# Attention by pairs of query blocks: two items per round, and a head's values ahead of the turning

## The chip, the cores and the metric

The kernel runs on one core of one Trainium2 chip. The core has engines that run side by side, each with its own queue in order: TensorE (matmuls, "PE" in the profile; its weight loads are "PEld"), VectorE ("DVE"), ScalarE ("ACT"), GpSimd ("POOL") and SyncE ("SP", which here only issues DMAs). The metric is device time of one execution in microseconds (us); lower is better. A profiled execution also gives a trace with start and length of every instruction.

## The reference

A hybrid encoder block: RMS norm, one input projection, stick-breaking attention and a gated linear recurrence (HGRN2) side by side on the same input, a gated merge, an MLP with squared ReLU and a last norm. Sequence 1024, width 1024, 8 attention heads of 64. What matters here is the attention, cut to its core:

```python
def block(args):                      # one block of 128 queries
    qi, i = args
    qpos = i * Q_BLOCK + jnp.arange(Q_BLOCK)
    z = jnp.einsum('bhqd,bhkd->bhqk', qi, k) * scale
    mask = kpos[None, :] < qpos[:, None]
    log_beta = jax.nn.log_sigmoid(z)
    log_rem = jnp.where(mask, log_beta - z, 0.0)
    between = lax.cumsum(log_rem, axis=3, reverse=True) - log_rem
    w = jnp.where(mask, jnp.exp(log_beta + between), 0.0)
    return jnp.einsum('bhqk,bhkd->bhqd', w, v)
```

So the weight of a key is a sigmoid times the product of what all later keys left over.

## The kernel before, in words

The kernel is written with a tile framework: the program states instructions and tiles, and a scheduler, when the program is built, fixes the order on each engine and gives each tile a place. Big SBUF tiles ([128, 1024]) come from a pool of 40 slots, [128, 512] tiles from a pool of 10 halves, and PSUM has 8 banks of [128, 512]. A tile that finds no free place waits until the last reader of an older one is done.

TensorE's order is bound by two lanes. `pe` (called by `matmul`, L121, and by `turn`, L821) chains each instruction behind the last one of its lane; `open_block` says which lane is open. "main" holds the attention's own products, "fill" the projections that are worked off beside it. A fill block must come behind the main block that ended two blocks ago (`AHEAD = 2`); otherwise the scheduler merges the lanes freely. `st.advance(n, upto)` emits n steps of fill (a step is two blocks of contraction, six matmuls of 512 columns, for most projections), `st.finish(j)` all steps up to job j.

An item is one head and one block of 128 queries. The 64 items go head by head, in each head in the order 7, 0, 6, 1, 5, 2, 4, 3 of query blocks, so that items with many keys (even places) and few keys (odd places) alternate. An item of query block qb has nk = (qb + 1) * 128 keys. It goes through four functions:

- `scores`: on TensorE z = q k in two products (QH and QL, high and low part), in banks of at most 512 keys; ScalarE writes two sigmoids of it, `rm` (L758) and `bt` (L761); POOL clears the last column of `bt` (L762).
- `weights`: VectorE scans `rm` from the last key to the first (L781) and multiplies it into `bt` (L157); SyncE copies the result by DMA to a new tile `wr` (L791). `weighted` remembers the last multiplication; the low part of a projection's keys (in `qk_epilogue`) is ordered behind it on VectorE.
- `turn`: TensorE transposes `wr` in blocks of 128 keys into a bank `pw` (L821), up to four blocks per bank; ScalarE copies the bank to `wT` (L144). It returns the head when all eight items of the head are turned.
- `values`: TensorE multiplies a head's `wT` with the values into two banks `po`, 44 records; ScalarE (L872, L874) and VectorE (L875) put them together in `osb`.

Before the loop, items 0 to 2 are scored and items 0 and 1 weighted. In iteration i the loop weights item i + 2, scores item i + 3, emits one or two steps of fill and turns item i. A head's `values` are emitted in the first turn of the next head: `turn` of query block 7 turns its upper four blocks, calls `between`, which runs `values`, and turns its lower four. `next(wsums)` (every second item) puts one transfer of the output weights on POOL's queue. `attended` holds the last `weighted` back for the splits of later weights.

Of the kernel before, what the change touches and what calls it, by code (L numbers as in the profile page):

```python
# [22 lines left out]
NT = T // P  # L23
# [16 lines left out]
def kernel(  # L40
# [37 lines left out]
    def slot_n(name, n, dt=F32):  # L78

        if n <= 512:  # L80
            return hpool.tile([P, 512], dt, tag="h", name=name)
        return slot(name, dt)

    def bank(name):
        return psum.tile([P, 512], F32, tag="p", name=name)
# [17 lines left out]
    def open_block(name):  # L103
        cur[0] = name
        lane = lanes[name]
        lane.gates = (lane.last,)
        if name == "main":
            lane.ends.append(lane.last)
        else:
            ends = lanes["main"].ends  # L110
            lane.gates += tuple(ends[-AHEAD : len(ends) - AHEAD + 1])
# [8 lines left out]
    def matmul(*a, **k):  # L120
        return pe(nc.tensor.matmul(*a, **k))  # L121
# [10 lines left out]
    last_lo, attended, silu = [None], [None], [None]  # L132
# [23 lines left out]
    def mul(out, a, b):  # L156
        return nc.vector.tensor_tensor(out=out, in0=a, in1=b, op=ALU.mult)  # L157
# [138 lines left out]
    def norm_transpose(acts, half, b0, n, between=None):  # L296
# [15 lines left out]
        if between:  # L312
            between()
# [210 lines left out]
    st = Stream()  # L524
# [200 lines left out]
    j_qk = {0: j_first}  # L725
# [9 lines left out]
    items = [(h, qb) for h in range(NHS) for qb in QB_ORDER]  # L735
    zs, wTt, seen = {}, {}, {}
    lastsel, weighted = [None], [None]

    def scores(h, qb):
        open_block("main")  # L740
        nk = (qb + 1) * P
        QH, QL, KS = qk[h]
        bt, rm = slot_n(f"bt{h}_{qb}", nk), slot_n(f"rm{h}_{qb}", nk)
        step = 320 if nk == 640 else 512
        for s0 in range(0, nk, step):
            m = min(nk - s0, step)
            n = max(m, 256)
            z = bank(f"z{h}_{qb}_{s0}")
            for i, Q in enumerate((QH, QL)):
                matmul(  # L750
                    z[:, :n],
                    Q[:, qb * P : (qb + 1) * P],
                    KS[:, s0 : s0 + n],
                    start=i == 0,
                    stop=i == 1,
                )
            c0, e = int(s0 == 0), m - (s0 + m == nk)
            nc.scalar.activation(  # L758
                rm[:, s0 + c0 - 1 : s0 + m - 1], z[:, c0:m], AF.Sigmoid, scale=-0.125
            )  # L760
            nc.scalar.activation(bt[:, s0 : s0 + e], z[:, :e], AF.Sigmoid, scale=0.125)  # L761
        lastsel[0] = nc.gpsimd.memset(bt[:, nk - 1 : nk], 0.0)  # L762
        zs[h, qb] = (bt, rm)
# [6 lines left out]
    def weights(h, qb):  # L770

        nk = (qb + 1) * P
        bt, rm = zs[h, qb]
        cut = qb == NT - 1
        parts = ((512, nk - 1), (0, 512)) if cut else ((0, nk - 1),)
        wr = slot_n(f"wr{h}_{qb}", nk, F32R)
        for i, (a, b) in enumerate(parts):
            rr = rm[:, a:b][:, ::-1]  # L780
            nc.vector.tensor_tensor_scan(  # L781
                out=rr,
                data0=rr,
                data1=bits[:, 1024 - nk + a : 1024 - nk + b][:, ::-1],
                initial=rm[:, b : b + 1] if i else 0.0,
                op0=ALU.mult,
                op1=ALU.max,
            )
            weighted[0] = mul(bt[:, a:b], bt[:, a:b], rm[:, a:b])
            cs = slice(a, nk if i == 0 else b)  # L790
            nc.sync.dma_start(wr[:, cs].bitcast(F32), bt[:, cs])  # L791
        zs[h, qb] = wr

    def turn(h, qb, between):

        open_block("main")
        wr = zs.pop((h, qb))
        qc, par = qb // 2, qb % 2
        nkb = 2 * qc + 2
        if (h, qc) not in wTt:  # L800
            wTt[h, qc] = [
                slot_n(f"wT{h}_{qc}_{k0}", 256 * min(nkb - k0, 4)).rearrange(
                    "p (k q) -> p k q", q=256
                )
                for k0 in range(0, nkb, 4)
            ]
        tiles = wTt[h, qc]
        qs = slice(par * P, (par + 1) * P)
        order = list(enumerate(tiles))
        for i, t in order[::-1] if qb == NT - 1 else order:  # L810
            n = min(qb + 1 - 4 * i, 4)
            if n <= 0:
                continue
            if qb == NT - 1 and i == 0:
                between()
                open_block("main")
            pw = bank(f"pw{h}_{qb}_{i}")
            for kb in range(n):
                s0 = (4 * i + kb) * P
                pe(  # L820
                    nc.tensor.transpose(  # L821
                        pw[:, kb * P : (kb + 1) * P].bitcast(F32R), wr[:, s0 : s0 + P], ident_r
                    )
                )
            hi_copy(t[:, 0:n, qs], pw[:, : n * P].rearrange("p (k q) -> p k q", q=P))
            turn_hi[0] = hi_last[0]
        seen[h] = seen.get(h, 0) + 1
        return (h,) if seen[h] == NT else None

    def values(h):  # L830


        open_block("main")
        whole, left, right = slice(0, 256), slice(0, P), slice(P, 256)
        pair, r = h // 2, (h % 2) * DHS
        if pair not in osb:
            osb[pair] = slot(f"osb{pair}")
        other = DHS - r
        pos = []
        for big in (3, 2):  # L840
            po = bank(f"po{h}_{big}")
            order = []
            for kb in range(0, 2 * big, 2):
                order += [(big, kb, 0, whole), (big, kb + 1, 1, whole)]
            order += [(big, 2 * big, 0, left), (big, 2 * big, 1, right)]
            few = 3 - big
            order += [(few, 0, 0, whole), (big, 2 * big + 1, 1, right)]
            if few:
                order += [(few, 1, 1, whole), (few, 2, 0, whole)]
            order += [(few, 2 * few + 1, 1, right)]  # L850
            ends = {}
            for i, (qc, kb, half, cs) in enumerate(order):
                ends.setdefault((qc, half), [i, i])[1] = i
            for i, (qc, kb, half, cs) in enumerate(order):
                c0 = 0 if qc == big else 256
                first, last = ends[qc, half]
                matmul(
                    po[half * DHS : (half + 1) * DHS, c0 + cs.start : c0 + cs.stop],
                    v_stat(h, kb),
                    wTt[h, qc][kb // 4][:, kb % 4, cs],  # L860
                    start=i == first,
                    stop=i == last,
                )
            pos.append((big, po))
        for big, po in pos:
            tmp = slot_n(f"ot{h}_{big}", 512)
            for qc, c0 in ((big, 0), (3 - big, 256)):
                wTt.pop((h, qc))
                n0 = P if qc == 0 else 0
                cs = slice(c0 + n0, c0 + 256)  # L870
                dst = osb[pair][r : r + DHS, qc * 256 : (qc + 1) * 256]
                nc.scalar.copy(tmp[r : r + DHS, cs], po[other : other + DHS, cs])  # L872
                if n0:
                    nc.scalar.copy(dst[:, 0:n0], po[0:DHS, c0 : c0 + n0])  # L874
                nc.vector.tensor_tensor(  # L875
                    out=dst[:, n0:],
                    in0=po[r : r + DHS, cs],
                    in1=tmp[r : r + DHS, cs],
                    op=ALU.add,
                )  # L880
# [1378 lines left out]
    n_fill = 9 * (j_hg[0] - j_qk[0]) + 18  # L2259
    n_first = 3  # L2260
    ready = deque()
    wsums = out_weight_sums()
    done = 0
    for i, it in enumerate(items):
        if i + 2 < len(items):
            weights(*items[i + 2])
        if i + 3 < len(items):
            st.finish(j_qk[items[min(i + 5, len(items) - 1)][0]])
            scores(*items[i + 3])
        if i % 2 == 1:  # L2270
            next(wsums, None)
        want = n_first + (i + 1) * (n_fill - n_first) // len(items)
        st.advance(want - done, j_hg[1])
        done = want
        before = ready.popleft() if ready else None

        def between():
            if before:
                values(*before)

        r = turn(*it, between)
        if i == len(items) - 2:
            attended[0] = weighted[0]
        if it[1] != NT - 1:
            between()
        if r:
            ready.append(r)
    while ready:
# [123 lines left out]
```

## Time and profile before

| | us |
|---|---|
| median of 3 runs | 1412.3 (1411.65 to 1412.98) |
| the profiled execution | 1413.22 |
| its span, first to last instruction | 1411.1 |
| TensorE busy | 1399.3 |
| VectorE, ScalarE, POOL busy | 1003.1, 684.3, 154.9 |

The attention loop takes the span from about 50 to 310 us; the linear recurrence, the merge and the output projection follow up to about 810, then the MLP. A matmul's record ends by a model, and the records of neighbours overlap, so a busy TensorE says little; the time from one start to the next says what an instruction took. Engine waits are given as "idle before <- what released it".

### The profile page before, as it was taken

What the parts mean: (1) busy time and instruction counts of PE and PEld (TensorE: products, weight loads), DVE (VectorE), ACT (ScalarE), POOL (GpSimd) and SP (SyncE); (2) the same over time, 40 slices, a digit from 0 to 9 for tenths busy, and PEclk for the clock granted to TensorE, in tenths of its full rate; (3) what the DMA queues carried; (4) which work ended last, traced back from release to release, by engine and by line L of the source; (5) the groups of instructions that cost most, each with busy time, mean ns of one, the idle gap of its engine ahead of it and who ended that gap; (6) DMA issues with size and microseconds to landing.
All of it is one profiled execution on the core that took longest, in us unless ns stands there. A gap on an engine that the chain in (4) does not pass through costs nothing. (4 is left out here: it accounts for less than half of the span.)

```text
span 1411.1 us, 22762 instructions
## 1 busy us (share of the span) xinstructions
PE 1399.3 (99%) x8782; PEld 1177.2 (83%) x8782; DVE 1003.1 (71%) x1332; ACT 684.3 (48%) x1207; POOL 154.9 (11%) x315
## 2 busy tenths in 40 slices
PE   9999999999999999999999999999999999999997
PEld 8888888988988888888888888888888888888886
DVE  6587687667556885966768896667666657768665
ACT  7576676644244453423354854444544433433343
POOL 3121121110112231000010200000000000000042
PEclk9999999999999999999999999999999999999999
DMA  7357365664254894555695524444436964686824
GB/s 213 97 169 194 113 166 152 141 156 135 69 163 137 261 252 159 187 183 177 202 297 179 194 86 146 149 165 164 151 134 241 362 239 173 259 292 229 285 92 176
DMA packets 166916, 258.94 MB, mean 183 GB/s; under 512 B 27500, under 2 KB 91544, under 8 KB 166808
## 3 DMA queue, kind: packets, MB, share of 16 engines
q1 hardware_dynamic: 148120, 205.31, 43.0%
q0 software_dynamic: 14080, 43.00, 11.7%
q10 hardware_dynamic: 4608, 9.18, 1.9%
q8 instruction: 69, 1.13, 0.3%
q14 instruction: 39, 0.32, 0.1%
HBM read 167.79 MB, written 70.78 MB: 169 GB/s over the span
## 5 line engine op out<-in xcount | busy, mean ns | idle before, releaser
L781 DVE TENSOR_TENSOR_SCAN rm<-rm,bits 128x511 f32<-128x511 f32 (+7 forms) x72 | 87.3, 1221 | 35.9 <-ACT rm L758 35.7
L144 ACT CAST whid<-w 128x1024 fp32r<-128x1024 f32 x30 | 31.6, 1053 | 155.0 <-PE pm L121 90.7
L121 PE MATMUL pm<-wlod,sh 128*128 128x512 f32 x240 | 93.5, 390 | 0.0
L121 PE MATMUL pm<-whid,sh 128*128 128x512 f32 x240 | 93.4, 389 | 0.0
L121 PE MATMUL pm<-whid,sl 128*128 128x512 f32 x240 | 93.4, 389 | 0.0
L121 PE MATMUL pm<-tl,sh 128*128 128x512 f32 (+1 forms) x210 | 81.3, 387 | 0.0
L121 PE MATMUL pm<-th,sl 128*128 128x512 f32 (+1 forms) x210 | 81.3, 387 | 0.0
L121 PE MATMUL pm<-th,sh 128*128 128x512 f32 (+1 forms) x210 | 81.3, 387 | 0.0
L149 DVE TENSOR_TENSOR wlod<-w,whid 128x1024 fp32r<-128x1024 f32 x30 | 36.7, 1222 | 59.3 <-ACT whid L144 59.3
L149 DVE TENSOR_TENSOR sl<-sa,sh 128x1024 fp32r<-128x1024 f32 x56 | 68.2, 1217 | 0.8 <-ACT sh L144 0.8
L2061 POOL TENSOR_SCALAR fss<-fss 128x1 f32<-128x1 f32 x8 | 4.5, 561 | 561.9 <-ACT fsc L2056 561.3
L144 ACT COPY wT<-pw 128x128 f32<-128x128 f32 (+3 forms) x96 | 44.1, 484 | 34.1 <-PE pw L821 28.6
L144 ACT CAST sh<-sa 128x1024 fp32r<-128x1024 f32 x56 | 57.2, 1046 | 5.2 <-DMA sa<-ad 3.7
L157 DVE TENSOR_TENSOR bt<-bt,rm 128x511 f32<-128x511 f32 (+7 forms) x72 | 48.9, 686 | 8.8 <-ACT bt L761 2.8
L121 PEld LDWEIGHTS pm<-wlod,sh 128*128 128x128 f32 x240 | 45.0, 188 | 9.8 <-DVE wlod L149 0.4
L121 PEld LDWEIGHTS pm<-whid,sh 128*128 128x128 f32 x240 | 45.1, 188 | 9.5
L121 PEld LDWEIGHTS pm<-whid,sl 128*128 128x128 f32 x240 | 45.0, 187 | 9.2
L758 ACT ACTIVATE rm<-z 128x511 f32<-128x511 f32 (+4 forms) x96 | 48.4, 506 | 4.5 <-DMA wr<-bt 2.4
L121 PE MATMUL pX<-sql,t1h 128*128 128x512 f32 x128 | 50.0, 391 | 0.4 <-DVE sql L149 0.3
L761 ACT ACTIVATE bt<-z 128x512 f32<-128x512 f32 (+3 forms) x96 | 48.7, 509 | 3.5 <-DMA wr<-bt 2.6
L121 PE MATMUL pX<-sqh,t1h 128*128 128x512 f32 x128 | 49.8, 389 | 0.0
L121 PE MATMUL pX<-sqh,t1l 128*128 128x512 f32 x128 | 49.8, 389 | 0.0
(922 smaller groups left out, 4346.6 us busy)
## 6 DMA issues: line engine op xcount, KB each, us to landing
w<-in_w_ff_dram SPq DMA_DIRECT2D x72, 512.0 KB, 4.6
sa<-ad SPq DMA_DIRECT2D x56, 512.0 KB, 6.7
ad<-a SPq DMA_DIRECT2D x32, 256.0 KB, 4.1
ad<-s SPq DMA_DIRECT2D x16, 512.0 KB, 3.1
tw<-in_w_out_dram POOLq DMA_DIRECT2D x24, 256.0 KB, 4.3
wr<-bt SPq DMA_DIRECT2D x24, 256.0 KB, 3.2
pr<-pd SPq DMA_DIRECT2D x10, 512.0 KB, 6.4
x<-in_x_dram SPq DMA_DIRECT2D x8, 512.0 KB, 9.2
```

The lines of the kernel that those rows point to most:

```text
L121: return pe(nc.tensor.matmul(*a, **k))
L144: hi_last[0] = after(in_turn("act", nc.scalar.copy(dst, src)), hi_behind[0])
L149: nc.vector.tensor_tensor(out=dst, in0=src, in1=hi.bitcast(F32), op=ALU.subtract),
L157: return nc.vector.tensor_tensor(out=out, in0=a, in1=b, op=ALU.mult)
L758: nc.scalar.activation(rm[:, s0 + c0 - 1 : s0 + m - 1], z[:, c0:m], AF.Sigmoid, scale=-0.125)
L761: nc.scalar.activation(bt[:, s0 : s0 + e], z[:, :e], AF.Sigmoid, scale=0.125)
L781: nc.vector.tensor_tensor_scan(out=rr, data0=rr, data1=bits[:, 1024 - nk + a : 1024 - nk + b][:, ::-1], initial=rm[:, b : b + 1] if i else ...
L2061: nc.gpsimd.tensor_scalar(out=ssq, in0=ssq, scalar1=1.0 / D, scalar2=EPS, op0=ALU.mult, op1=ALU.add)
```

## The change

The loop goes over pairs. Round i (even) weights item i + 2, scores items i + 3 and i + 4, weights item i + 3, emits the fill of two items, runs the values of the head that the round before completed, and turns items i and i + 1. `turn` no longer takes `between`, and all its banks follow each other. `finish` looks one item further (i + 6 instead of i + 5), as the round scores up to item i + 4. `next(wsums)` comes once per round, and `attended` is set at the head of the last round.

```diff
-    def turn(h, qb, between):
+    def turn(h, qb):
...
-            if qb == NT - 1 and i == 0:
-                between()
-                open_block("main")
             pw = bank(f"pw{h}_{qb}_{i}")
...
-    for i, it in enumerate(items):
+    for i in range(0, len(items), 2):
         if i + 2 < len(items):
             weights(*items[i + 2])
-        if i + 3 < len(items):
-            st.finish(j_qk[items[min(i + 5, len(items) - 1)][0]])
-            scores(*items[i + 3])
-        if i % 2 == 1:
-            next(wsums, None)
-        want = n_first + (i + 1) * (n_fill - n_first) // len(items)
+            st.finish(j_qk[items[min(i + 6, len(items) - 1)][0]])
+            for it in items[i + 3 : i + 5]:
+                scores(*it)
+            weights(*items[i + 3])
+        else:
+            attended[0] = weighted[0]
+        next(wsums, None)
+        want = n_first + (i + 2) * (n_fill - n_first) // len(items)
         st.advance(want - done, j_hg[1])
         done = want
-        before = ready.popleft() if ready else None
-
-        def between():
-            if before:
-                values(*before)
-
-        r = turn(*it, between)
-        if i == len(items) - 2:
-            attended[0] = weighted[0]
-        if it[1] != NT - 1:
-            between()
+        if ready:
+            values(*ready.popleft())
+        for it in items[i : i + 2]:
+            r = turn(*it)
         if r:
             ready.append(r)
```

## The prediction

> **What bounds the kernel now.** I read the page first, then the windows by stage, then what TensorE waited for, then the timeline of TensorE inside attention.
>
> ```profile
> PE 1399.3 (99%) x8782; PEld 1177.2 (83%) x8782; DVE 1003.1 (71%) x1332; ACT 684.3 (48%) x1207; POOL 154.9 (11%) x315
> ...
> PEclk9999999999999999999999999999999999999999
> ```
>
> TensorE is busy for 1399.3 of 1411.1 us at full clock, and the clock row has no dip. So anything that does not shorten TensorE's own sequence can at best remove the few places where it stops. Attention runs from about 50 to 310 us:
>
> ```profile
> 50.00:310.00 260.00, 258.75 (x1738) 222.37 (x1738) 189.08 (x240) 170.64 (x407) 44.82 (x125) 1.00 0.58 153
> 310.00:771.00 461.00, 460.76 (x3864) 385.64 (x3864) 326.26 (x490) 188.90 (x337) 60.37 (x99) 1.00 0.59 186
> ```
>
> Columns after the length are busy time (and count) of PE, PEld, DVE, ACT and POOL, then clock, DMA share and GB/s. In attention VectorE has 189 and ScalarE 171 of 260 us, so neither is the bound. The next stage is as full on TensorE (460.76 of 461), so a microsecond won in attention is passed on to the end, and so is one lost. What TensorE waited for between 40 and 320 us is one row of 0.8 us (for the values' PSUM bank) and one of 0.4 us (for a landed weight tile):
>
> ```profile
> PE pjv L121 <- DVE osb L875: 0.8, 1, 0.8
> PE pw L821 <- DMA wr<-bt: 0.4, 1, 0.4
> ```
>
> Busy time hides more, because matmul records overlap. So I compare starts. One iteration today is turn, scores, fill:
>
> ```profile
> 199.68 0.64 PE L821 MATMUL pw<-ident_r,wr 128*128 128x128 f32 x6
> 200.15 0.46 PE L121 MATMUL z<-KS,QH 128*128 128x512 f32 x1
> 200.45 0.39 PE L121 MATMUL z<-KS,QL 128*128 128x512 f32 x1
> 200.68 0.40 PE L121 MATMUL z<-KS,QH 128*128 128x512 f32 x1
> 200.91 0.40 PE L121 MATMUL z<-KS,QL 128*128 128x512 f32 x1
> 201.15 0.39 PE L121 MATMUL pjqk<-xnh,wqk7h 128*128 128x512 f32 x1
> ```
>
> Columns are start, length, instruction. A 512-wide product takes 0.23 us from start to start, but the first score behind the transposes takes 0.30. Six transposes take 0.47, 0.078 each. A score block that follows fill pays nothing (0.23 at once):
>
> ```profile
> 49.84 0.40 PE L121 MATMUL z<-KS,QH 128*128 128x512 f32 x1
> 50.07 0.40 PE L121 MATMUL z<-KS,QL 128*128 128x512 f32 x1
> 50.31 0.39 PE L121 MATMUL z<-KS,QH 128*128 128x512 f32 x1
> ```
>
> So leaving a run of transposes costs 0.07 to 0.08 us. That is the one thing in TensorE's sequence that the change touches.
>
> **The change, part by part.** *Seams from transposes to scores.* Today scores(4) to scores(63) each follow a turn: 60 seams. With two turns and two scores per round the scores of rounds 2 to 60 follow turns: 30 seams. The price over the whole stage, from the groups by shape:
>
> ```profile
> L121 PE MATMUL z<-KS,QH 128*128 128x512 f32 x40 | 17.9, 447 | 0.0
> L121 PE MATMUL z<-KS,QL 128*128 128x512 f32 x40 | 15.7, 393 | 0.0
> ...
> L121 PE MATMUL z<-KS,QH 128*128 128x256 f32 x24 | 7.7, 322 | 0.0
> ...
> L121 PE MATMUL z<-KS,QL 128*128 128x256 f32 x24 | 6.7, 281 | 0.0
> ...
> L121 PE MATMUL z<-KS,QH 128*128 128x384 f32 x16 | 5.8, 365 | 0.0
> L121 PE MATMUL z<-KS,QL 128*128 128x384 f32 x16 | 5.4, 338 | 0.0
> L121 PE MATMUL z<-KS,QH 128*128 128x320 f32 x16 | 5.4, 342 | 0.0
> L121 PE MATMUL z<-KS,QL 128*128 128x320 f32 x16 | 4.8, 307 | 0.0
> ```
>
> QH and QL do the same work; QH is longer by 2.2 + 1.0 + 0.4 + 0.6 = 4.2 us. Over 60 seams that is 0.07 each, as in the timeline. Thirty fewer: 2.1 us by the groups, 2.4 by 0.08 from the timeline. I take **-2.2 us**.
>
> [...]
>
> ```profile
> 286.30 0.80 PEld L821 LDWEIGHTS pw<-ident_r,wr 128*128 128x128 f32 x7
> ...
> 287.05 0.19 PEld L121 LDWEIGHTS z<-KS,QH 128*128 128x128 f32 x1
> 287.08 0.38 PE L121 MATMUL z<-KS,QH 128*128 128x320 f32 x1
> ```
>
> The scores' load starts at 287.05, 0.03 us ahead of its own matmul and behind the whole chain of transposes' loads. [...]
>
> *Seams to fill.* At the tail three turns go straight to fill, at the same price (0.30, then 0.23):
>
> ```profile
> 294.34 0.46 PE L121 MATMUL pjq<-xnh,wq1h 128*128 128x512 f32 x1
> 294.64 0.39 PE L121 MATMUL pjq<-xnl,wq1h 128*128 128x512 f32 x1
> 294.87 0.40 PE L121 MATMUL pjq<-xnh,wq1l 128*128 128x512 f32 x1
> ```
>
> In pairs one such seam is left of three: -0.1 us.
>
> *Values ahead of the turning.* Today the values sit between the two halves of a head's first turn:
>
> ```profile
> 182.14 0.46 PE L821 MATMUL pw<-ident_r,wr 128*128 128x128 f32 x4
> 182.53 4.12 PE L121 MATMUL po<-wT,V 128*64 128x256 f32 x44
> 186.58 0.54 PE L821 MATMUL pw<-ident_r,wr 128*128 128x128 f32 x4
> ```
>
> Four transposes ahead of the values take 0.39, 0.08 above 4 x 0.078. Seven of eight such seams go (-0.5); the way from values back to transposes stays. In their place stands fill to values, which no row shows: between nothing (fill to scores, above) and 0.08 each, or 0.6 in all. A gain below nothing is excluded, since the 44 records themselves stay. I take the middle, +0.3.
>
> *Where scores, weights and forced fill move.* Per round VectorE gets the same scans, ScalarE the same sigmoids, SyncE the same `wr` transfers, POOL the same memsets and `tw` transfers, one `next(wsums)` per round instead of per second item; none of it adds work. `finish` now looks two items ahead of the second score, and forces three steps of head 1's projection early instead of one; steps taken early are only missing later, where fill is plentiful. Cost nothing; without that cover each step is 6 x 0.23 = 1.4 us.
>
> *The added wait.* weights(i+3) now stands directly behind scores(i+3) and scores(i+4), so its scan waits for ScalarE within the round, and behind it on VectorE wait the projections' low parts (ordered after `weighted`), then the `Q` copies on POOL. The item is turned one round later, behind two fills of about four steps (2 x 24 x 0.23 = 11 us) plus turns and scores: some 13 us, against the 12.1 us between these two rows for item 63 today:
>
> ```profile
> 290.61 0.47 PE L121 MATMUL z<-KS,QH 128*128 128x512 f32 x1
> ...
> 302.68 0.51 PE L821 MATMUL pw<-ident_r,wr 128*128 128x128 f32 x4 [0.42 <-DMA wr<-bt]
> ```
>
> The even items get another round, about 20 us. So the turn should not come to wait oftener than now. The stops of today are 1.14 us where 0.17 is due, in front of this row (the z before it starts at 125.46 and is 384 wide):
>
> ```profile
> 125.46 0.34 PE L121 MATMUL z<-KS,QL 128*128 128x384 f32 x1
> 126.60 0.35 PE L121 MATMUL pjv<-wv1h,xnh 128*128 128x256 f32 x1 [0.81 <-DVE osb L875]
> ```
>
> (384 of 512 columns of 0.23), so 1.0, and the 0.4 in front of the last turn: 1.4 us together. In pairs such stops lie between none and several us (the slot rival prices those), since one round with values now wants more banks within 3 us: two for `po`, three for the turns, three for the scores and one for fill, nine of eight. I take 1.7, near the rows of today, so +0.3.
>
> *Sum:* -2.2 - 0.1 - 0.5 + 0.3 + 0.3 = **-2.2 us**. The profiled execution took 1413.2 us (span 1411.1 and 2.1 around it), which would become 1411.0; the median of the three runs is 1412.3, and from it I forecast **1410.1 us**.
>
> **The rivals.** *The stops go as well.* If values, turns and scores in longer blocks give the banks back in time, the 1.4 us of stops and my 0.3 vanish: -2.5 - 1.4 = -3.9, 1408.4. For it: ScalarE is idle for a third of the stage. Against: nine banks of eight.
>
> [...]
>
> *Slower: SBUF holds the second score up.* The pair needs one more `bt`, `rm` and `wr` at a time, out of 40 slots. ScalarE already waits for a slot at the second item of heads 6 and 7:
>
> ```profile
> ACT bt L761 <- DMA wr<-bt: 2.6, 1, 2.6
> ACT rm L758 <- DMA wr<-bt: 2.4, 1, 2.4
> ```
>
> TensorE did not stop for these. In pairs the weight tile that would free the slot is read only at the round's end, one fill of 24 x 0.23 = 5.5 us later, so such a wait becomes 2.5 + 5.5 = 8 us with two score banks held, ScalarE's queue stuck, and the copies that free the other banks behind it. Cover is one fill, 5.5 us, so each costs TensorE some 2.5 us. One such wait eats the gain; from two on beyond what the seams give (-2.5 + 5 = +2.5) it is slower, with three 1412.3 + 5 = 1417. [...]
>
> **How the numbers follow.** The forecast case (1409 to 1411.5) has 0.44, the stops gone 0.19, the change without effect 0.16, the slots 0.21. About 0.2%, or 2.8 us, is what a measurement can tell from no change. Faster than that (under 1409.5): all of the second case and 0.21 of the first, 0.40. Slower (over 1415.1): 0.19 of the slots. Within: 0.41. The range goes from 1407.6, just under the case without stops, to 1416, short of three slot waits; about 0.1 is left out on each side. The forecast's own range is 1409.0 to 1411.5.
>
> **What would show it.** Right: pairs of `pw` groups with no score between them, QH longer than QL by about 2.1 instead of 4.2 us in all, values starting behind fill. The slots: new rows "PE <- ACT" or "PE <- DMA wr" and ScalarE waits for `wr` above 5 us. Without effect: fill between two `pw` groups of a round. The prediction is wrong if TensorE's starts show more than 3 us of new stops in attention, or if a later stage loses what attention wins.

## The result and the profile after

| | before | after |
|---|---|---|
| median, us (6 runs each) | 1412.45 (1411.57 to 1414.26) | 1422.18 (1421.40 to 1424.23) |
| span of the profiled execution | 1411.1 | 1420.1 |
| TensorE busy | 1399.3 | 1402.1 |

The ratio is 1.0071, with a 95% interval of 1.0058 to 1.0084: 9.7 us slower, where 2.2 us faster was forecast. TensorE does the same work (8782 records in both). What it waited for, in the view of its waits after the change (us in total, times, longest):

```profile
PE z L121 <- DVE osb L872: 3.7, 1, 3.7
...
PE z L121 <- ACT bt L761: 1.6, 1, 1.6
PE z L121 <- ACT v L914: 1.2, 2, 0.7
```

All are waits of a score (`z`) for something that is not its operand. VectorE's addition of the values (`osb`) and ScalarE's sigmoids and copies (`bt`, `v`) are the readers of older PSUM banks, and a score needs a free bank to write to. So these are waits for a bank. In attention TensorE's timeline has them at these places (start, length, instruction):

```profile
116.68 0.40 PE L121 MATMUL z<-KS,QH 128*128 128x512 f32 x1
116.92 0.39 PE L121 MATMUL z<-KS,QL 128*128 128x512 f32 x1
118.92 0.39 PE L121 MATMUL z<-KS,QH 128*128 128x256 f32 x1 [1.62 <-ACT bt L761]
...
277.38 0.28 PE L121 MATMUL z<-KS,QL 128*128 128x256 f32 x1
278.40 0.50 PE L121 MATMUL z<-KS,QH 128*128 128x512 f32 x1 [0.74 <-ACT v L914]
...
288.94 0.31 PE L121 MATMUL z<-KS,QL 128*128 128x320 f32 x1
292.98 0.61 PE L121 MATMUL z<-KS,QH 128*128 128x320 f32 x1 [3.73 <-DVE osb L872]
293.39 0.47 PE L121 MATMUL z<-KS,QL 128*128 128x320 f32 x1
293.65 0.63 PE L121 MATMUL pjq<-xnh,wq1h 128*128 128x512 f32 x1
294.08 0.63 PE L121 MATMUL pjq<-xnl,wq1h 128*128 128x512 f32 x1
...
298.67 0.39 PE L121 MATMUL pjq<-xnh,wq1h 128*128 128x512 f32 x1
298.90 0.39 PE L121 MATMUL pjq<-xnl,wq1h 128*128 128x512 f32 x1
```

Each of these stops, and a fourth of 0.6 us at 255 us, stands in front of a bank of the round's second score. From 293.65 the 512-wide products start 0.43 us apart instead of 0.23: the granted clock had gone from 1.00 to 0.50 during the stop of 4 us, at 291.7 us by windows of 0.2 us. The windows show it (length, busy PE, PEld, DVE, ACT, POOL, then clock, DMA share, GB/s):

```profile
286.00:292.00 6.00, 3.25 (x33) 2.54 (x29) 1.80 (x3) 0.15 (x2) 0.80 (x2) 0.98 0.94 262
292.00:293.00 1.00, 0.02 (x1) 0.05 (x1) 0.34 (x2) 0.94 (x4) 1.00 (x5) 0.50 0.70 265
293.00:298.60 5.60, 5.60 (x14) 4.54 (x15) 4.05 (x6) 3.74 (x10) 2.04 (x4) 0.51 0.92 164
298.60:304.00 5.40, 5.40 (x30) 4.54 (x30) 1.45 (x3) 2.68 (x6) 0.00 (x0) 1.00 0.42 125
```

Why did the bank come free so late at 292? VectorE's timeline, and ScalarE's:

```profile
290.08 0.69 DVE L1214 TENSOR_TENSOR wga8r<-wga8r,wga8r 128x512 f32<-128x512 f32 x1 [4.88 <-DMA wga8r<-in_w_in_dram]
290.81 0.69 DVE L1214 TENSOR_TENSOR wga8r<-wga8r 128x512 f32<-128x512 f32 x1
291.53 0.42 DVE L872 TENSOR_TENSOR osb<-po,ot 64x256 f32<-64x256 f32 x1
```

```profile
285.77 0.37 ACT L869 COPY ot<-po 64x256 f32<-64x256 f32 x1 [2.91 <-PE po L121]
291.99 0.26 ACT L869 COPY ot<-po 64x128 f32<-64x128 f32 x1 [5.84 <-DVE osb L872]
```

VectorE took its instructions in order: the first addition, whose copy ScalarE had ready at 286.14 us (285.77 + 0.37), started at 291.53, behind both differences. These two, of a gate's weights (`wga8r`) that nobody needs yet, stand in front of the additions and wait 4.9 us for a load of 512 KB, issued at 283.10 us; from 286 to 292 us the DMA engines' share is 0.94. Behind them the additions of head 6 wait, ScalarE's next copy waits for the additions (5.8 us), and the `po` bank that the second score is to take stays full.

At 278 us ScalarE's queue is what holds a bank. One of its sigmoids waits 3.3 us for a transfer of `wr`, which is the wait for an SBUF slot that the prediction describes, and the copy that frees the bank (`v`) stands behind it:

```profile
277.04 0.98 ACT L758 ACTIVATE rm<-z 128x511 f32<-128x511 f32 x2 [3.32 <-DMA wr<-bt]
277.90 0.44 ACT L914 COPY v<-pji 128x128 f32<-128x128 f32 x2
```

At 118 us a cast of ScalarE stands in the same way ahead of the sigmoids (`bt`) that free the bank; the last experiments come to it.

**Account.** I took, for every product between the first score and the last values, how far the next start lies beyond the product's own time (0.226 us for 512 columns and in proportion, 0.095 and 0.057 for the records of the values). Seams of turns and values together cost 14.9 us before and 14.3 after: -0.6. Single stops of over 0.2 us: 1.6 before, 7.4 after: +5.9. Half clock: +2.2 (2.4 with the last score in it, as below). Behind attention, stops at 496, 501 and 1101 us against one at 507: +1.3. With 0.3 us at the start that is 9.1 of the 9.0 us between the spans.

### The profile page after: what moved, and what is told of

Same layout as the page of the kernel before. It is cut to its first block, busy times and chain, and to the rows that moved or that the text cites. A ratio compares the mean times of both kernels' runs of the same rounds, so it can differ in the third digit from the quotient of the medians.

```text
span 1420.1 us, 22753 instructions
## 1 busy us (share of the span) xinstructions
PE 1402.1 (99%) x8782; PEld 1179.5 (83%) x8782; DVE 1005.2 (71%) x1332; ACT 682.7 (48%) x1207; POOL 153.7 (11%) x315
## 5 line engine op out<-in xcount | busy, mean ns | idle before, releaser
L144 ACT COPY wT<-pw 128x128 f32<-128x128 f32 (+3 forms) x96 | 40.8, 487 | 19.1 <-PE pw L818 13.9
```

Of the source, the lines that this page charges most:

```text
L144: hi_last[0] = after(in_turn("act", nc.scalar.copy(dst, src)), hi_behind[0])
```

## The experiments

Two theories. **Q, a queue:** the differences in front of the additions make the big stop (3.9 us, 0.3 at the next product, 2.4 at half clock). **B, banks:** two scores in a row want three banks at once, and whoever holds a bank a little long stops TensorE. All ratios are against the kernel before on the same chip; some of the runs come from different chips, so small differences between the medians of two runs say little.

**The differences behind the additions** (`e1_adds_first`). `put_together` is the last addition of the values:

```diff
-            sub(b0, b0, a0)
+            after(sub(b0, b0, a0), put_together[0])
```

> Theory Q (a queue): in the changed kernel VectorE's differences of the first raw gate unit (wga8r) stand in front of head 6's additions and wait for a late transfer, so the values' PSUM bank comes free late; that one place costs TensorE 3.9 us of stop, 0.3 us at the next product and 2.4 us at half clock, 6.5 of the 9.7 us. This kernel only puts those two differences behind the additions. Q expects 1422.2 - 6.5 = 1415.7 us and no stop near 289 us. Theory B (banks: two scores in a row want three banks at once) expects that another wait takes the place and 1419 us or more is left.

Measured: 1417.37 us, ratio 1.0035 (1.0021 to 1.0049). The stop near 289 us and the half clock are gone, and 4.8 us with them. But another stop in front of a second score grew: at 118 us from 1.8 to 3.0 us, behind a cast on ScalarE that waited 2.4 us for its load. And a stop of 1.4 us is new, in front of a product that waits for a transfer of its own operand `QL`, which neither theory covers:

```profile
74.78 0.47 PE L121 MATMUL z<-KS,QL 128*128 128x512 f32 x1 [1.22 <-DMA QL<-QL]
...
117.70 0.39 PE L121 MATMUL z<-KS,QL 128*128 128x512 f32 x1
120.92 0.39 PE L121 MATMUL z<-KS,QH 128*128 128x256 f32 x1 [2.83 <-ACT bt L762]
```

So Q is real and is about one half; 5 us are left without it. Neither theory met its number: Q had said 1415.7 us, B 1419 us or more.

**The second score apart** (`e2_scores_apart`). The rest is the changed kernel:

```diff
-            for it in items[i + 3 : i + 5]:
-                scores(*it)
+            scores(*items[i + 3])
             weights(*items[i + 3])
...
-        st.advance(want - done, j_hg[1])
+        part = (want - done) // 2
+        st.advance(part, j_hg[1])
+        if i + 4 < len(items):
+            scores(*items[i + 4])
+        st.advance(want - done - part, j_hg[1])
```

> The second score of a round is put behind half of the round's fill; the rest is the changed kernel. Theory B: all four stops stand in front of the second score's banks (1.8, 0.6 with 0.3, 0.9 and 3.9 us, with 2.4 at half clock), so all go: 1411 to 1413 us. Theory Q: the three small stops go (3.6 us), the bank held by the additions still stops TensorE near 289 us, at the next instruction that needs a bank: 1417 to 1419 us.

Measured: 1412.18 us, ratio 0.9998 (0.9989 to 1.0007). The whole loss is gone, with the differences still in front of the additions:

```profile
285.60 0.69 DVE L1214 TENSOR_TENSOR wga8r<-wga8r,wga8r 128x512 f32<-128x512 f32 x1 [2.28 <-DMA wga8r<-in_w_in_dram]
286.33 0.69 DVE L1214 TENSOR_TENSOR wga8r<-wga8r 128x512 f32<-128x512 f32 x1
287.05 0.41 DVE L872 TENSOR_TENSOR osb<-po,ot 64x256 f32<-64x256 f32 x1
```

```profile
285.50 0.34 PE L121 MATMUL z<-KS,QL 128*128 128x384 f32 x1
...
288.41 0.30 PE L121 MATMUL z<-KS,QH 128*128 128x320 f32 x1
```

VectorE waits for its load here too, but TensorE asks for the next score bank 3 us later, after a stretch of fill that needs none, and does not stop. The run is not quite clean, for VectorE's wait is also shorter, 2.3 us instead of 4.9. Counted from the start of the values before it, the bank of the stop is wanted after 8.3 us instead of 5.6, and the addition that frees it ends after 7.9 us instead of 9.3. So of the 3.9 us the distance takes away some 2.7, and the load that lands sooner the rest. B fits best; Q is what it meets in one place.

**Both edits** (`e3_both`).

> Both edits: differences behind the additions, scores apart. If the two theories share the loss (6.5 to Q, 3.6 to B), 1411 to 1412 us, at or just under the kernel before, with the seams' net gain of about 1 us. If a third cause holds a part, such as the values' place or the SBUF slots, over 1414 us is left.

Measured: 1411.64 us, ratio 1.0002 (0.9993 to 1.0011). With the scores apart the order on VectorE no longer matters. A third cause of the size that was expected (over 1414 us) is not there; a smaller one could hide in the interval, about 1 us to either side.

**The values alone** (`e4_values_front`). In the kernel before, `values` is called ahead of `turn` and no longer inside it.

> The kernel before, single items, with only the values moved in front of a head's first turn. Q and B both expect no loss: 1412 to 1413 us, for one item per round wants one or two score banks and the additions stay where they were. If the values' new place is a cause by itself, 1414 us or more and a stop behind the values.

Measured: 1413.52 us, ratio 1.0009 (1.0000 to 1.0018). By the medians the values' place costs 1.3 us, by the interval between nothing and 2.5. The row of the waits is the last turn, not a bank; it is 1.3 us longer than before:

```profile
PE pw L818 <- DMA wr<-bt: 1.7, 1, 1.7
```

**The scores alone** (`e5_scores_pair`). The kernel before with

```diff
-        if i + 3 < len(items):
-            st.finish(j_qk[items[min(i + 5, len(items) - 1)][0]])
-            scores(*items[i + 3])
+        if i % 2 == 0 and i + 3 < len(items):
+            st.finish(j_qk[items[min(i + 6, len(items) - 1)][0]])
+            for nxt in items[i + 3 : i + 5]:
+                scores(*nxt)
```

> The kernel before with one part of the change alone: two items are scored in a row in every second iteration; turns stay single and the values between the halves of a head's first turn. Theory B (two scores in a row want three banks at once) expects stops in front of second scores here too, 2 to 6 us: 1414 to 1418 us. If the banks only run out because turns and values come in a block with the scores, it stays at 1412 to 1413 us.

Measured: 1418.54 us, ratio 1.0044 (1.0027 to 1.0061). Turns are single, values stand where they stood, and 6 us are lost, by a stop of 2.9 us at the known place, one of 1.7 us at 254 us in front of a bank of fill, and some 1.5 us at half clock:

```profile
276.89 0.28 PE L121 MATMUL z<-KS,QL 128*128 128x256 f32 x1
279.89 0.49 PE L121 MATMUL z<-KS,QH 128*128 128x512 f32 x1 [2.72 <-ACT wT L144]
```

Both stops end with a copy of ScalarE (`wT`) that came late because ScalarE had waited for a transfer of `wr`: 3.5 us for the copy itself at the first, and 6.1 us for a sigmoid ahead of it at the second:

```profile
278.38 0.98 ACT L758 ACTIVATE rm<-z 128x511 f32<-128x511 f32 x2 [6.11 <-DMA wr<-bt]
```

So two scores in a row are too many for the banks by themselves, and here the wait for an SBUF slot is what holds them.

**One bank less.** `keep_warm(1)` behind the loop keeps the warm-up's bank until then; once in the kernel before (`e6_bank_held`), once with the scores apart (`e7_apart_bank_held`).

> The kernel before, but the bank of the warm-up products is kept until attention is over (one more such product there), so attention has seven banks instead of eight. If banks are what is scarce (B), stops in front of z, pw or fill appear here as well, 3 us or more: over 1415 us. If one bank is to spare in the kernel before, 1412 to 1413 us, and then the three banks of two scores are more than the one that was free.

Measured: 1414.52 us, ratio 1.0011 (1.0001 to 1.0022). Single scores get by with seven banks, and no bank wait of 0.2 us or more shows in attention. The 2 us are lost at the last turn, which waits for its `wr` for 2.0 us instead of 0.4, and at half clock behind it (1.4 us). The kernel before has about one bank to spare.

> Scores apart by half of the fill (e2_scores_apart), with the same bank held: seven banks. B expects that taking a bank away brings the stops back that taking the second score away removed: 1415 us or more. If the scores' lateness and not the bank made the stops, it stays near 1412 us.

Measured: 1418.42 us, ratio 1.0038 (1.0023 to 1.0053), 0.4% or some 6 us above the same kernel with eight banks. The stops are back, the longest (3.1 us) now in front of a bank of fill behind the first score:

```profile
116.35 0.28 PE L121 MATMUL z<-KS,QL 128*128 128x256 f32 x1
119.55 0.58 PE L121 MATMUL pjv<-wv1h,xnh 128*128 128x256 f32 x1 [2.92 <-ACT bt L761]
```

So the bank is the resource, and not the time at which the score comes. Turns in pairs use the spare one. Scores in pairs are too many even with single turns, as the run before these two shows.

**Two steps of fill fewer** (`e8_same_fill`: `+ 16` for `+ 18` in `n_fill`, on top of both edits).

> Both edits of e3_both, and two steps of fill fewer in the loop, since this loop forces three steps early where the kernel before forces one. In e3_both the product behind pgq at 499 us waits 1.1 us for ScalarE; if that came from the two steps by which the later stage is out of phase, it goes: 1410.5 to 1411.5 us. If not, as e3_both, 1411.6 to 1412.2.

Measured: 1416.38 us, ratio 1.0022 (1.0012 to 1.0032): a miss. The wait at 499 us went, but others came in attention. The longest stop, 2.8 us, stands in front of a score that meets the end of a projection whose bank VectorE had not read, since ScalarE's part of the same reading (`q`) had waited 8.6 us for a transfer of `wr`:

```profile
PE z L121 <- DVE q L157: 2.6, 1, 2.6
```

A stop of 1.2 us at 280 us is new too. Where fill and scores meet is as tight as that: with the scores apart and eight banks the loop still lost 4.7 us by two steps of 1.4 us. So the distance between the scores is no cure by itself.

**ScalarE's casts behind the sigmoids** (`e10_casts_behind`; the last run, `e11_before_casts`, has them in the kernel before). Two stops at 119 to 121 us were left with the scores apart. ScalarE's timeline there:

```profile
114.47 0.98 ACT L758 ACTIVATE rm<-z 128x511 f32<-128x511 f32 x2 [1.60 <-DVE bt L157]
117.62 1.05 ACT L144 CAST wqk6h<-wqk6r 128x1024 fp32r<-128x1024 f32 x1 [2.18 <-DMA wqk6r<-in_w_in_dram]
118.58 0.97 ACT L761 ACTIVATE bt<-z 128x512 f32<-128x512 f32 x2
```

It is the same pattern as on VectorE: a cast that waits for its load stands ahead of the sigmoids that free two score banks. The edit, in `Unit.split`, where `last_bt` is the last sigmoid emitted:

```diff
+                was, hi_behind[0] = hi_behind[0], hi_behind[0] or last_bt[0]
                 lo = after(after(hi_lo(h, l, r), last_lo[0]), attended[0])
+                hi_behind[0] = was
```

> e3_both, with ScalarE's casts of the next weights put behind the last sigmoid emitted so far. In e2_scores_apart and e3_both two stops are left at 119 to 121 us (0.4 and 1.3 us) where a cast that waits for its load stands in front of the sigmoids that free two score banks. If that order is their cause, they go: 1410 to 1411 us, 0.1% under the kernel before. If the banks are merely scarce there, they stay or move: 1412 us.

Measured: 1410.43 us, ratio 0.9986 (0.9977 to 0.9996), with turns in pairs, scores apart and both orders: 1.8 us under the kernel before and some 12 under the change. No wait of TensorE is left in attention; in the view of its waits over the whole program the longest are:

```profile
PE warm L121 <- POOL ident masks.py:199: 2.2, 1, 2.2
PE pho L121 <- issue: 0.7, 1, 0.7
```

> The kernel before with the casts alone put behind the sigmoids. Its one stop of 1.0 us at 126 us goes if the same cast makes it: 1411 to 1412 us; otherwise unchanged at 1412.4 us. It tells whether a gain of e10_casts_behind belongs to the pairs.

Measured: 1411.95 us, ratio 0.9999 (0.9989 to 1.0008). The stop at 126 us went, the last turn's wait grew (0.9 us), and the total stayed. So the casts alone bring nothing that can be told from no change. The stops of over 0.2 us in attention are 1.6 us before, 1.1 here and none with the pairs of turns. That accounts for most of the gain; why the last turn does not wait in pairs was not tried.

## Why the prediction was wrong, point by point

- **"What bounds the kernel" held.** TensorE's own sequence sets the time; what attention lost reached the end whole. But the busy shares that ruled VectorE and ScalarE out (189 and 171 of 260 us) are averages of the stage, and said nothing of how late one reading can come.
- **The seams, -2.5 us, were mis-sized: -0.6.** Most of the scores' part came, -1.6 of -2.2: QH is longer than QL by 2.6 us in all after the change (0.7 + 1.2 + 0.5 + 0.2, where the restarts behind stops are counted in), against 4.2.

```profile
L121 PE MATMUL z<-KS,QH 128*128 128x512 f32 x40 | 16.4, 410 | 0.7 <-ACT v L914 0.7
...
L121 PE MATMUL z<-KS,QL 128*128 128x512 f32 x40 | 15.7, 392 | 0.0
```

  What I left out is that the transposes themselves depend on what stands ahead (before, four of them up to the next score took 0.29 or 0.30 us behind fill and 0.37 or 0.38 behind the values) and on how many they are. Before, two transposes behind fill took 0.12 us up to the next score, 0.06 each:

```profile
290.49 0.29 PE L821 MATMUL pw<-ident_r,wr 128*128 128x128 f32 x2
290.61 0.47 PE L121 MATMUL z<-KS,QH 128*128 128x512 f32 x1
```

  and seven took 0.55 (the rows from 286.53 to 287.08). After, nine in a row take 0.73:

```profile
199.09 0.89 PE L818 MATMUL pw<-ident_r,wr 128*128 128x128 f32 x9
199.82 0.46 PE L121 MATMUL z<-KS,QH 128*128 128x512 f32 x1
```

  0.73 against 0.12 + 0.55 = 0.67: 0.06 per round, some 2 us over 32 rounds. I priced all at 0.078.
- **Values behind fill** cost 0.09 each (93.18 to 93.50, 0.32 instead of 0.23), just above the upper bound given.

```profile
93.18 0.39 PE L121 MATMUL pjqk<-xnh,wqk3l 128*128 128x512 f32 x1
93.50 4.12 PE L121 MATMUL po<-wT,V 128*64 128x256 f32 x44
```

- **The step that failed is "I take 1.7, near the rows of today, so +0.3".** I had counted nine banks of eight, and then priced their lack by a kernel that scores one item at a time. Measured: 7.4 us of stops instead of 1.7, and 2.2 at half clock. The prediction's own sign of being wrong, more than 3 us of new stops, came. The rows of before had no case of the demand that the change makes, so their stops were no bound for it; the price was to be had from the holders of a bank, which the same trace shows waiting for transfers by microseconds: ScalarE's waits of 2.4 and 2.6 us for `wr` that I quoted, and one of a cast for its load, which I did not:

```profile
ACT wqk6h L144 <- DMA wqk6r<-in_w_in_dram: 3.3, 1, 3.3
```

- **"Its turn should not come to wait oftener" held:** no wait of a turn for `wr` appears after the change.
- **"Cost nothing" for the fill forced early** was not tried alone. `e8_same_fill` shows that the loop's time can hang on two steps of fill by 4.7 us.
- **The rival of the slots** had the right side, and named banks held by a stuck queue as its last link. It was not the whole: the stop of 3.9 us came through VectorE and a load, and slot waits alone did not stop TensorE. They cost it nothing before (2.4 and 2.6 us), nor in `e10_casts_behind` (9.8 us in three waits, the longest 5.2). But where the banks ran out, such waits held them: 0.9 us in the changed kernel, both stops of `e5_scores_pair` and the longest of `e8_same_fill`. A version with more SBUF slots was not tried, so how much of the loss more slots would save is open.
- **Luck.** `e10_casts_behind` ends at 1410.4 us, beside the forecast of 1410.1. That bears nothing out: the forecast kept 1.7 us of stops and won 2.5 by seams, and that kernel has no stop left and three edits more.
- **The case without effect** (0.16) did not come: after the change the nine transposes of a round follow each other, as in the row at 199.09 us.
- **The clock** I had only as "no dip": a stop as long as this one was outside what the rows of before could show.

## What to carry to other kernels

Before work is put in blocks, count the PSUM banks that the block wants at once, and compare with what is free in the tightest round, not with the stops of the old order. Hiding is bought with distance between requests for a bank: with half of the fill between the two scores the whole loss of 9.7 us went, and with the same fill behind both it stood. The distance has to be looked at again after each edit, since two steps of fill fewer brought stops back. In an engine's queue, whatever waits for a load should stand behind what frees a bank: that was worth 4.8 us on VectorE.

## What the runs showed of the hardware

Behind four stops TensorE's granted clock was about half. In the changed kernel it fell during the stop of 3.9 us (288.94 to 292.98, less one product): by windows of 0.2 us it is 1.00 up to 291.6 us and 0.50 from 291.8 to 298.4 us, 6.8 us at half clock with the two windows at the ends (0.77 and 0.67). There 11 products took 0.43 us each instead of 0.23. The other three stops were of 3.1 us (`e7_apart_bank_held`, 256-wide products 0.21 us apart behind it instead of 0.12), 2.9 (`e5_scores_pair`, 0.25 and 0.21 instead of 0.12) and only 2.2 (`e6_bank_held`, in front of the last turn):

```profile
302.97 0.51 PE L821 MATMUL pw<-ident_r,wr 128*128 128x128 f32 x4 [2.02 <-DMA wr<-bt]
```

```profile
304.00:306.00 2.00, 2.00 (x14) 1.25 (x12) 0.00 (x0) 0.09 (x1) 0.00 (x0) 0.50 0.06 24
```

Behind a stop of 3.0 us the clock stayed at 1.00; in `e1_adds_first`, around the stop at 118 us:

```profile
117.00:122.00 5.00, 2.17 (x16) 1.66 (x16) 2.72 (x2) 2.64 (x5) 0.65 (x2) 1.00 0.67 191
```

So it did behind the changed kernel's stops of 1.8, 0.6 and 0.9 us (1.00 from 116 to 122, from 254 to 258 and from 276 to 282 us). In `e8_same_fill`, with a stop of 2.8 us, the run's mean granted clock is 0.997, against 0.998 or 0.999 of the kernel before on that chip. In `e5_scores_pair` the half clock shows only after TensorE had gone on: it went on at 279.89 us, the 512-wide product at 280.22 still took 0.24, and the 256-wide one at 280.46 took 0.25.

So the length of a stop did not decide by itself here: the clock was half behind one of 2.2 us and full behind one of 3.0 us. What else decides, no run here shows. What can be carried on is the measured price: 1.4 us at half clock on top of a stop of 2.2 us, and 2.2 us on top of one of 3.9.
